# One decoder layer on one core: the seventh product of each weight pair moved behind the next pair's first, layer norm two pairs earlier, attention-output tiles rehoused

## The chip, the cores and the metric

The kernel runs on one core of one Trainium2 chip. The metric is device time in microseconds of one launch. The kernel before takes 1314.48 us, the median of three runs (1313.3 to 1315.68).

## What is computed

One layer of 1024 tokens by 1024 channels, float32, between two RMS norms. The normalised input `h` goes through one wide projection whose columns are cut into eleven pieces:

```python
h = _rmsnorm(x, norm_g)
q, k, v, o_pre, i_pre, f_pre, z_a, glu_in, z_b, ga_pre, gb_pre = split(h @ w_in)
q, k = silu(_causal_dwconv(concat(q, k), conv_qk_w, conv_qk_b))       # 4 taps
hm = _mlstm(q, k, v, i_pre + b_i, f_pre + b_f)                        # 4 heads of 256
out_a = sigmoid(o_pre) * headnorm(hm) * mhn_g * silu(z_a)
u = glu_in[..., :D_B] * sigmoid(glu_in[..., D_B:])
u = _causal_dwconv(u, dw_w, dw_b)                                     # 31 taps
u = silu(_layernorm(u, ln_g, ln_b)) * silu(z_b)
merged = sigmoid(ga_pre) * (out_a @ w_pa) + sigmoid(gb_pre) * (u @ w_pb)
out = _rmsnorm(x + merged @ w_out, final_g)
```

Every large matrix product is made exact to float32 by splitting each operand into a high and a low part and adding three passes (high by high, high by low, low by high).

## The kernel before, in words

**The projection.** `h` is turned, split and kept in SBUF as `hb`, four blocks of 512 inputs by 512 tokens, with three sums of blocks in `ext`. The columns of `w_in` are worked off in 40 jobs: the first six are four heads of `v` and the pairs gb0 and ga0 in plain form, and then come 34 "pairs" of 128-column tiles in the order of the table `ORDER` (jobs 6 to 39; names in the trace carry the job's number). `run_job` loads the raw weights of the next job, steps the generator `prep` of the next job (it splits the weights into `hi` and `lo`, the tags a, t, s and b standing for the weight blocks and for two pairs of sums; for t, s and b the low part is made on POOL's queue by an accumulating DMA), and issues the products of its own job in `quad`.

**A pair.** `quad` (L411) computes the four 512-token quarters of two column tiles from seven products instead of eight. `product` (L405, matmul L408) is twelve matmuls of 128 by 128 by 512 into one PSUM bank. In the order of the code: p1 into bank X, p2 into Z, p3 on top of X, p4 into W, p5 on top of X, p6 on top of Z, p7 on top of X. Between them X and Z are read out: ACT copies X after p1 (L431) and after p3 (L437) and Z after p2 (L434); DVE adds W (L441), then X after p5 (L445), then Z (L449). A product into a bank waits until the reader of that bank has finished, so p3 waits for L431, p5 for L437 and p7 for L445; between p5 and p7 stands p6 alone. `emit` then applies the pair's activation and stores.

**The 31-tap convolution.** The pairs ga0 to ga3 each give two tiles `u` to DVE, which needs 31 instructions of a whole tile each (L517 once, L519 30 times) into one accumulator `acc`; they are issued at low priority, so that the scheduler puts them where DVE has room. The accumulator is stored to `c_dram` (L520), and added into `s_dram` by an accumulating DMA on POOL's queue (L524). There is one `acc` buffer: the next tile's L517 waits until that DMA has read it.

**Layer norm** of the convolution, `layer_norm` (L595), is a generator that `run_job` steps beside a job's products, from pair `LN_AT` = 28 on (job 34). It loads the sum `s`, takes the mean on TensorE (`tstat`, `trow`), then goes twice over eight tiles: the first pass sums squares, the second scales each tile, applies SiLU, multiplies by `z` and stores to `u_dram`. A tile `ct` is loaded in `centred` (L589) and used at once. The tiles f, qr, qa and `z` share the tag `tmp` of five buffers.

**mLSTM and the last three products.** `stages` (L893) issues 16 chunks (four heads by four), whose outputs `gate` are stored to `oa_dram` (L884). Between stages `y_b` (L908) issues matmuls of yb, eight tiles, each multiplied by sgb (L912) and stored to `m1_dram`. When the chunks are done, `oa_tile` (L941) loads each of eight tiles `oar` from `oa_dram` and splits it into `oa` (ACT, L106, then DVE, L107). `oar` shares the tag `st`, two buffers, with sgb and sga. Then follow ya (`oa` by w_pa), `mrg`, and out (by w_out) with the final norm.

Instructions of one engine run in the order in which the Tile scheduler has put them; DMAs are issued by SP in its order, accumulating ones by POOL. PSUM is held as four banks `ms`, and four banks `qb` while the pairs run.

Of the kernel before, what the change touches and what calls it, by code (L numbers as in the profile page):

```python
# [9 lines left out]
F32 = mybir.dt.float32  # L10
F32R = mybir.dt.float32r
AF = mybir.ActivationFunctionType
ALU = mybir.AluOpType
# [28 lines left out]
         "zb0 zb1 zb2 zb3 o3 za3 mb3 ma3")  # L42
LN_AT = 28


@with_exitstack
def kernel(ctx: ExitStack, tc: tile.TileContext, x, norm_g, w_in, b_if, conv_qk_w, conv_qk_b,
# [13 lines left out]
    dpool = ctx.enter_context(tc.tile_pool(name="dpool", bufs=1, space=DRAM))  # L61
    ms_pool = ctx.enter_context(tc.tile_pool(name="ms_pool", bufs=4, space=PSUM))
    pj_cm, pj_pool = pool("pj_pool", bufs=2, space=PSUM)
    state = {}
    state["pj"] = pj_pool

# [344 lines left out]
    def quad(n, dst, emit):  # L411
# [17 lines left out]
        product(X, a11, b11, True, False)  # L429
        yield  # L430
        nc.scalar.copy(dst(0, 0), X)  # L431
        product(Z, s1, t1, True, False)
# [17 lines left out]
        emit(0, 1, dst(0, 1), False)  # L450
        product(X, a22, t4, False, True)
        yield
        emit(1, 0, X, True)

# [133 lines left out]

    def centred(c, n):  # L589
        ct = state["cv"].tile([P, KD - 1 + S], F32, tag="u", name=f"ct{n}_{c}", bufs=2)[:, 0:S]  # L590
        nc.sync.dma_start(ct, c_dram[c])
        nc.vector.tensor_tensor(ct, ct, state["mu"], op=ALU.subtract)
        return ct

    def layer_norm():  # L595
# [8 lines left out]
        mu = state["cv"].tile([P, S], F32, tag="acc", name="mu", bufs=1)  # L604
        state["mu"] = mu
        to_row(st, 0, mu)
        yield
        yield
        for c in range(KT):
            ct = centred(c, 0)  # L610
            if c == 0:
                nc.scalar.activation(sv, ct, AF.Square)
            else:
                nc.scalar.activation(ct, ct, AF.Square)
                nc.vector.tensor_tensor(sv, sv, ct, op=ALU.add)
            yield
# [5 lines left out]
        to_row(st, 1, sv)  # L622
        yield
        for c in range(KT):
            ct = centred(c, 1)
            z = state["tmp"].tile([P, S], F32, tag="tmp", name=f"z{c}", bufs=5)
            nc.sync.dma_start(z, z_dram[c])
            nc.vector.tensor_tensor(ct, ct, sv, op=ALU.mult)
            nc.scalar.activation(ct, ct, AF.Silu, bias=lb(c), scale=lg(c))
            nc.vector.tensor_tensor(z, z, ct, op=ALU.mult)  # L630
            nc.sync.dma_start(u_dram[c], z)
            yield
# [29 lines left out]
    close(pj_cm)  # L662
    qb_cm, state["qb"] = pool("qb", bufs=4, space=PSUM)
    lns_cm, lns = pool("lns", reuse_waits="tile")
# [225 lines left out]
    def stages():  # L890

        at = lambda i, s: chunks[i][s] if 0 <= i < len(chunks) else None
        for i in range(len(chunks) + 2):  # L893
            for f in (at(i - 1, "v"), at(i - 1, "u"), at(i + 2, "l"), at(i, "s"), None, at(i, "k"), at(i + 1, "p"), None,
                      at(i - 2, "f"), None, at(i, "i")):
                yield f

    u2 = []

    def u2_tile(c):  # L900
# [4 lines left out]
        u2.append(ut)  # L905

    def y_b():
        for d in range(KT):  # L908
            sg = yp.tile([P, S], F32, tag="st", name=f"sgb{d}", bufs=2)
            nc.sync.dma_start(sg, sgb_dram[d])  # L910
            ps = yield from proj(d, f"yb{d}", rhs=lambda k, sl: (u2[k][:, 0, sl], u2[k][:, 1, sl]))
            nc.vector.tensor_tensor(sg, ps, sg, op=ALU.mult)  # L912
            nc.sync.dma_start(m1_dram[d], sg)

# [53 lines left out]
    for d in range(KT):  # L968
        i = KT + d
        sg = yp.tile([P, S], F32, tag="st", name=f"sga{d}", bufs=2)  # L970
        nc.sync.dma_start(sg, sga_dram[d])
        m1 = yp.tile([P, S], F32, tag="m1", name=f"m1_{d}", bufs=2)
        nc.sync.dma_start(m1, m1_dram[d])
        ps = run(proj(i, f"ya{d}", rhs=lambda k, sl: (oa[k][:, 0, sl], oa[k][:, 1, sl])), i)
        mt = u2p.tile([P, 2, S], F32R, tag="u2", name=f"mrg{d}", bufs=KT)
        for hf in range(2):
            sl = slice(hf * 512, (hf + 1) * 512)
            nc.vector.tensor_tensor(sg[:, sl], ps[:, sl], sg[:, sl], op=ALU.mult)  # L978
            nc.vector.tensor_tensor(sg[:, sl], sg[:, sl], m1[:, sl], op=ALU.add)
            split(mt[:, 0, sl], mt[:, 1, sl], sg[:, sl])  # L980
# [90 lines left out]
```

## Time and profile before

| | us |
|---|---|
| median of three runs | 1314.48 |
| profiled execution, whole | 1314.68 |
| its span | 1312.9 |
| PE busy | 1219.8 (93%) |
| DVE busy | 929.5 (71%) |
| ACT busy | 638.6 (49%) |
| POOL busy | 142.0 (11%) |
| DMA moved | 217.89 MB, mean 166 GB/s |
| mean granted TensorE clock | 0.971 |

Span is from the first to the last instruction; the 1.8 us between it and the whole time lie around it. A matmul's shown duration overlaps the next one's, so that products are measured from start to start. In rows of a timeline, a bracket at the end gives the time the engine sat idle before the row and what ended that. A clock of 1.00 is TensorE's level of 2.4 GHz, and 0.5 the level of 1.2 GHz; a mean between them says how the two were mixed.

### The profile page before, as it was taken

To read this page: it belongs to the slowest core of one execution; us is meant where nothing else is said; L and a number is where in the kernel's file an instruction comes from. 1 tells how busy PE (TensorE), PEld (TensorE's weight loads), DVE (VectorE), ACT (ScalarE), POOL (GpSimd) and SP (SyncE) were. 2 spreads that over 40 slices of the span, in tenths; PEclk is the share of its full clock that TensorE was granted. 3 is DMA by queue.
4 is the path that set the end of the run, shared out by engine and by line. 5 is a ranking of instruction groups with operands and counts; after the bars stand their busy time and mean duration, and the time that the engine had idled before them with its cause. 6 is when DMAs were issued, how large, how long until landed. Compare 5 with 4: busy or idle time off the path is not lost. (4 is left out here: it accounts for less than half of the span.)

```text
span 1312.9 us, 16737 instructions
## 1 busy us (share of the span) xinstructions
PE 1219.8 (93%) x6228; PEld 1019.6 (78%) x6228; DVE 929.5 (71%) x1207; ACT 638.6 (49%) x948; POOL 142.0 (11%) x252
## 2 busy tenths in 40 slices
PE   8999999999989999999989988786898998899996
PEld 7889987887777877877868867665787886688996
DVE  6699899469789898989889455746787753444442
ACT  6522356646554474645646455566655531321223
POOL 1100011111111111111101111001111110000002
PEclk9999999999999999999989998897999998999998
DMA  8201577756765777666666977978877535443403
GB/s 263 65 1 59 167 172 169 197 129 144 174 159 132 163 166 175 147 143 163 164 167 172 247 204 209 290 228 260 244 229 227 168 109 188 151 142 135 170 17 129
DMA packets 170640, 217.89 MB, mean 166 GB/s; under 512 B 10177, under 2 KB 135481, under 8 KB 170558
## 3 DMA queue, kind: packets, MB, share of 16 engines
q1 hardware_dynamic: 154862, 168.58, 40.4%
q0 software_dynamic: 15696, 48.24, 20.0%
q8 instruction: 49, 0.80, 0.2%
q14 instruction: 33, 0.27, 0.1%
HBM read 117.67 MB, written 54.55 MB: 131 GB/s over the span
## 5 line engine op out<-in xcount | busy, mean ns | idle before, releaser
L519 DVE SCALAR_TENSOR_TENSOR acc<-u,dww,acc 128x1024 f32<-128x1024 f32 x240 | 307.7, 1282 | 3.7
L116 PE MATMUL v<-hi,hb 128*128 128x256 f32 (+1 forms) x512 | 94.5, 288 | 2.4 <-ACT hb L106 1.9
L116 PE MATMUL ya<-oa,whi 128*128 128x512 f32 x256 | 86.2, 413 | 9.2 <-ACT oa L106 5.7
L116 PE MATMUL out<-whi,mrg 128*128 128x256 f32 x512 | 91.0, 281 | 0.0
L116 PE MATMUL yb<-u,whi 128*128 128x512 f32 x256 | 85.3, 410 | 3.0 <-ACT u L106 1.7
L116 PEld LDWEIGHTS v<-hi,hb 128*128 128x128 f32 x512 | 80.3, 193 | 3.5 <-ACT hb L106 2.5
L116 PEld LDWEIGHTS out<-whi,mrg 128*128 128x128 f32 x512 | 78.6, 188 | 0.0
L116 PE MATMUL out<-wlo,mrg 128*128 128x256 f32 x256 | 71.9, 281 | 0.0
L116 PE MATMUL v<-lo,hb 128*128 128x256 f32 (+1 forms) x256 | 71.2, 286 | 0.0
L116 PEld LDWEIGHTS ya<-oa,whi 128*128 128x128 f32 x256 | 49.0, 194 | 27.7 <-ACT oa L106 9.4
L467 ACT ACTIVATE f<-f 128x512 f32<-128x512 f32 x69 | 43.1, 630 | 39.3 <-DVE f L445 24.3
L106 ACT CAST whi<-wr 128x1024 fp32r<-128x1024 f32 x24 | 25.2, 1050 | 74.9 <-PE ya L116 57.4
L489 DVE SCALAR_TENSOR_TENSOR qa<-qr,par,qa 128x1023 f32<-128x1023 f32 (+2 forms) x48 | 59.5, 1279 | 0.0
L116 PEld LDWEIGHTS yb<-u,whi 128*128 128x128 f32 x256 | 45.7, 190 | 12.4 <-ACT u L106 2.3
L116 PE MATMUL ya<-oa,wlo 128*128 128x512 f32 x128 | 52.0, 406 | 0.0
L116 PE MATMUL yb<-u,wlo 128*128 128x512 f32 x128 | 50.5, 394 | 0.0
L116 PEld LDWEIGHTS v<-lo,hb 128*128 128x128 f32 x256 | 48.5, 193 | 0.0
L116 PEld LDWEIGHTS out<-wlo,mrg 128*128 128x128 f32 x256 | 48.2, 188 | 0.0
L212 DVE TENSOR_TENSOR sum<-raw 128x512 f32<-128x512 f32 x34 | 23.4, 689 | 34.7 <-ACT f L437 6.9
L978 DVE TENSOR_TENSOR sga<-ya,sga 128x512 f32<-128x512 f32 x16 | 10.3, 686 | 45.9 <-PE ya L116 45.9
L208 DVE TENSOR_TENSOR sum<-raw 128x512 f32<-128x512 f32 x34 | 23.4, 689 | 24.9 <-ACT lo10b L193 3.5
L1023 ACT ACTIVATE junk<-res 128x256 f32<-128x256 f32 x32 | 13.4, 418 | 48.9 <-DVE res L1022 42.4
(1561 smaller groups left out, 3373.2 us busy)
## 6 DMA issues: line engine op xcount, KB each, us to landing
raw<-in_w_in_dram SPq DMA_DIRECT2D x144, 256.0 KB, 4.0
ct<-c_dram SPq DMA_DIRECT2D x16, 512.0 KB, 5.3
xt<-in_x_dram SPq DMA_DIRECT2D x8, 512.0 KB, 4.3
raw<-in_w_in_dram SPq DMA_DIRECT2D x8, 512.0 KB
v_dram<-vt SPq DMA_DIRECT2D x8, 512.0 KB, 2.9
c_dram<-acc SPq DMA_DIRECT2D x8, 512.0 KB
q_dram<-qa SPq DMA_DIRECT2D x8, 512.0 KB
sgb_dram<-f SPq DMA_DIRECT2D x8, 512.0 KB, 8.3
```

Of the source, the lines that this page charges most:

```text
L106: ins = nc.scalar.copy(hi, src)
L116: nc.tensor.matmul(ps, a, b, start=(first and j == 0), stop=(last and j == len(todo) - 1))
L208: nc.vector.tensor_tensor(sm[0][:, 0], raw[:, 0], raw[:, 3], op=ALU.add)
L212: nc.vector.tensor_tensor(sm[1][:, 0], raw[:, 0], raw[:, 1], op=ALU.add)
L467: nc.scalar.activation(t[j][:, HF[hf]], src, func, scale=sgn(neg))
L489: nc.vector.scalar_tensor_tensor(acc[j][:, s:], raw[j][:, 0:S - s], cw(KQ - 1 - s, t), acc[j][:, s:], op0=ALU.mult, op1=ALU.add)
L519: nc.vector.scalar_tensor_tensor(acc, u[:, k:k + S], dw(k, c), acc, op0=ALU.mult, op1=ALU.add)
L978: nc.vector.tensor_tensor(sg[:, sl], ps[:, sl], sg[:, sl], op=ALU.mult)
L1023: nc.scalar.activation(junk, r, AF.Square, accum_out=ss[:, t, n:n + 1])
```

## The change

Four things, all in the one function.

1. `quad` no longer issues p7. It leaves a closure `tail` (p7 and the emit of that quarter), which the next pair calls after its own p1. To let X live on beside the next pair's X, Z and W, `qb` gets six banks; `ms` has two in that time (`ms2_pool`), and four again after it (`ms3_pool`).
2. `LN_AT` is 26, so layer norm is stepped from job 32 on; `load_c` issues the loads of `ct` and `z` one step ahead of their use. Layer norm has one less step per pair to advance in, since a pair has one yield less.
3. The `oa` tiles get places of their own in reverse order, `oar` gets two buffers of its own, the first three `oa_tile` are issued as soon as the chunks' pools are closed, and yb's tiles 6 and 7 stay in SBUF (`m1k`) instead of going through `m1_dram`.
4. `stages` ends one round earlier and issues the last chunk's finish straight behind.

```diff
-LN_AT = 28
+LN_AT = 26
...
         product(X, a11, b11, True, False)
         yield
+        if state["tail"]:
+            state["tail"]()
         nc.scalar.copy(dst(0, 0), X)
...
-        product(X, a22, t4, False, True)
-        yield
-        emit(1, 0, X, True)
+
+        def tail():
+            product(X, a22, t4, False, True)
+            emit(1, 0, X, True)
+        state["tail"] = tail
...
-    def centred(c, n):
+    def load_c(c, n):
+        if c >= KT:
+            return None, None
         ct = state["cv"].tile([P, KD - 1 + S], F32, tag="u", name=f"ct{n}_{c}", bufs=2)[:, 0:S]
         nc.sync.dma_start(ct, c_dram[c])
-        nc.vector.tensor_tensor(ct, ct, state["mu"], op=ALU.subtract)
-        return ct
+        z = None
+        if n:
+            z = state["tmp"].tile([P, S], F32, tag="tmp", name=f"z{c}", bufs=5)
+            nc.sync.dma_start(z, z_dram[c])
+        return ct, z
...
+        ahead = load_c(0, 1)
         for c in range(KT):
-            ct = centred(c, 1)
-            z = state["tmp"].tile([P, S], F32, tag="tmp", name=f"z{c}", bufs=5)
-            nc.sync.dma_start(z, z_dram[c])
+            ct, z = ahead
+            ahead = load_c(c + 1, 1)
+            nc.vector.tensor_tensor(ct, ct, mu, op=ALU.subtract)
...
-    qb_cm, state["qb"] = pool("qb", bufs=4, space=PSUM)
+    close(ms_cm)
+    ms_cm, state["ms"] = pool("ms2_pool", bufs=2, space=PSUM)
+    qb_cm, state["qb"] = pool("qb", bufs=6, space=PSUM)
...
-        for i in range(len(chunks) + 2):
+        for i in range(len(chunks) + 1):
...
+        yield chunks[-1]["f"]
...
+            if state.get("oap"):
+                m1[d] = state["oap"].tile([P, S], F32, name=f"m1k{d}")
+                nc.vector.tensor_tensor(m1[d], ps, sg, op=ALU.mult)
+            else:
...
-    oa = [None] * KT
+    state["oap"] = oap
+    oa = [oap.tile([P, 2, S], F32R, name=f"oa{d}") for d in range(KT - 1, -1, -1)][::-1]
 
     def oa_tile(d):
-        oa[d] = oap.tile([P, 2, S], F32R, name=f"oa{d}")
-        raw = yp.tile([P, S], F32, tag="st", name=f"oar{d}", bufs=2)
+        raw = oap.tile([P, S], F32, tag="oar", name=f"oar{d}", bufs=2)
...
+    for _ in range(3):
+        oa_tile(todo.pop(0))
```

How the instructions move, in three places. First PE where pair 15 (k1) ends and pair 16 (mb1) begins, x, z and w being the banks X, Z and W of the pair whose number they carry; before:

```order
L408 MATMUL z15_2955<-hb_98,hi15s_2916 128x512 x2
L408 MATMUL z15_2955<-hb_98,lo15s_2917 128x512
L408 MATMUL x15_2954<-ext_779,hi15b_2937 128x512 x2
L408 MATMUL x15_2954<-ext_779,lo15b_2938 128x512
...
L408 MATMUL x16_3092<-hb_98,hi16a_3008 128x512 x2
L408 MATMUL x16_3092<-hb_98,lo16a_3009 128x512
```

and in the change:

```order
L407 MATMUL z15_2944<-hb_98,lo15s_2921 128x512
L407 MATMUL x16_3077<-hb_98,hi16a_3012 128x512 x2
L407 MATMUL x16_3077<-hb_98,lo16a_3013 128x512
...
L407 MATMUL x15_2943<-ext_783,hi15b_2929 128x512 x2
L407 MATMUL x15_2943<-ext_783,lo15b_2930 128x512
...
L407 MATMUL z16_3078<-hb_98,hi16t_3033 128x512 x2
L407 MATMUL z16_3078<-hb_98,lo16t_3034 128x512
...
L407 MATMUL w16_3137<-hb_98,hi16a_3012 128x512 x2
L407 MATMUL x16_3077<-ext_783,hi16t_3033 128x512 x2
```

Product p7 of pair 15 (x15 from hi15b and lo15b) now stands behind pair 16's p1, and so does every pair's. The last two rows show a second move: the first two matmuls of w stand ahead of p3, which the scheduler does in seven pairs (7, 13, 16, 21, 24, 28 and 31). On DVE the start of the next accumulator (L517 before, L520 now) stands ahead of the read of X after p5 in pair 15, as before; in pair 22, where it also stood ahead, it now stands behind.

Second, PE where the mean of the convolution is taken (tstat0, from the loaded sum s1); before, in pair 34 (zb2):

```order
L408 MATMUL w34_5662<-hb_98,hi34a_5541 128x512 x2
L408 MATMUL w34_5662<-hb_98,lo34a_5542 128x512
L577 MATMUL tstat0_5683<-ones_86,s1_5659 128x2 x8
L408 MATMUL x34_5618<-ext_779,hi34s_5584 128x512 x2
L408 MATMUL x34_5618<-ext_779,lo34s_5585 128x512
```

and in the change, where pair 34 begins:

```order
L407 MATMUL z33_5499<-hb_98,lo33s_5479 128x512
L407 MATMUL x34_5650<-hb_98,hi34a_5572 128x512 x2
L580 MATMUL tstat0_5425<-ones_86,s1_5401 128x2 x8
L407 MATMUL x34_5650<-hb_98,lo34a_5573 128x512
L407 MATMUL x34_5650<-hb_98,hi34a_5572 128x512
L586 MATMUL trow0_5458<-ident_81,tst0_5434 8x128
```

The mean has moved from behind p4 of pair 34 into its p1, ahead of p7 of pair 33.

Third, SP where the oa tiles are loaded; before:

```order
L884 DMA oa_dram_71<-gate2_3_8703 128x2x256
L913 DMA m1_dram_74<-sgb6_8839 128x1024
L703 DMA wr11_9103<-in_w_pa_dram 128x8x128
L943 DMA oar0_8979<-oa_dram_71 128x1024
L884 DMA oa_dram_71<-gate3_3_8817 128x2x256
L913 DMA m1_dram_74<-sgb7_8906 128x1024
L943 DMA oar1_8986<-oa_dram_71 128x1024
L703 DMA wr12_9171<-in_w_pa_dram 128x8x128
L943 DMA oar2_8991<-oa_dram_71 128x1024
```

and in the change:

```order
L900 DMA oa_dram_71<-gate2_3_8711 128x2x256
L900 DMA oa_dram_71<-gate3_3_8825 128x2x256
L966 DMA oar0_8917<-oa_dram_71 128x1024
L966 DMA oar1_8921<-oa_dram_71 128x1024
L996 DMA sga0_9028<-sga_dram_72 128x1024
L719 DMA wr11_9111<-in_w_pa_dram 128x8x128
L966 DMA oar2_8925<-oa_dram_71 128x1024
L966 DMA oar3_8935<-oa_dram_71 128x1024
L966 DMA oar4_8945<-oa_dram_71 128x1024
L996 DMA sga1_9096<-sga_dram_72 128x1024
L719 DMA wr12_9179<-in_w_pa_dram 128x8x128
L966 DMA oar5_8955<-oa_dram_71 128x1024
```

The last two chunks' stores stand next to each other, the loads of oar stand ahead of what waits for yb's last tiles (the stores to m1_dram of tiles 6 and 7 are gone), and the loads of sga0 and sga1 and of the weights wr11 and wr12 stand between them.

## Rows read from the trace of the kernel before

**Rows 1.** Windows: stretch, length, PE, PEld, DVE, ACT, POOL busy, PEclk, DMA share, GB/s
```profile
162.88:736.66 573.78, 553.54 (x2354) 443.68 (x2353) 487.37 (x504) 320.42 (x407) 80.76 (x96) 0.99 0.68 163
736.66:888.05 151.39, 129.96 (x539) 102.53 (x537) 79.29 (x88) 84.26 (x104) 16.40 (x18) 0.93 0.82 234
...
1105.60:1132.53 26.93, 17.89 (x44) 9.59 (x44) 11.95 (x10) 8.23 (x8) 0.00 (x0) 0.75 0.60 194
```

**Rows 2.** Waits of PE at L408: us in total, times, longest us
```profile
PE x L408 <- DVE qr L445: 11.7, 5, 5.1
PE x L408 <- DVE f L445: 10.1, 6, 3.8
```

**Rows 3.** Timeline of PE, p7 of pairs 15, 30, 33; what follows
```profile
364.62 1.22 PE L408 MATMUL x<-ext,hi15b 128*128 128x512 f32 x2 [5.08 <-DVE qr L445]
...
368.87 0.63 PE L408 MATMUL x<-hb,hi16a 128*128 128x512 f32 x2
...
672.75 1.22 PE L408 MATMUL x<-ext,hi30b 128*128 128x512 f32 x2 [4.04 <-DVE qr L445]
...
678.04 0.71 PE L408 MATMUL x<-hb,hi31a 128*128 128x512 f32 x2
...
733.86 0.63 PE L408 MATMUL x<-ext,hi33b 128*128 128x512 f32 x2
...
736.66 0.63 PE L408 MATMUL x<-hb,hi34a 128*128 128x512 f32 x2
```

**Rows 4.** Waits of DVE at L517
```profile
DVE acc L517 <- DMA s_dram<-acc: 17.1, 5, 7.1
```

**Rows 5.** Timeline of DVE in pair 15
```profile
361.83 0.81 DVE L517 TENSOR_SCALAR acc<-u,dww,par 128x1024 f32<-128x1024 f32 x1 [7.09 <-DMA s_dram<-acc]
```

**Rows 6.** Timelines of POOL and SP, from the convolution's end
```profile
728.51 0.87 POOL L524 DMA_DIRECT2D s_dram<-acc  x1 [8.27 <-DVE acc L519]
735.32 0.34 SPq L599 DMA_DIRECT2D s<-s_dram  x1
738.56 0.87 POOL L194 DMA_DIRECT2D lo34b<-raw  x1 [0.96 <-DMA s<-s_dram]
```

**Rows 7.** Timeline of PE, the waits of pairs 35, 36 and 39
```profile
767.17 1.22 PE L408 MATMUL x<-ext,hi35t 128*128 128x512 f32 x2 [3.54 <-ACT f L431]
774.74 0.72 PE L408 MATMUL x<-ext,hi35s 128*128 128x512 f32 x2 [0.32 <-ACT f L437]
781.55 0.73 PE L408 MATMUL x<-ext,hi35b 128*128 128x512 f32 x2 [1.01 <-DVE f L445]
806.97 1.22 PE L408 MATMUL x<-ext,hi36b 128*128 128x512 f32 x2 [3.80 <-DVE f L445]
847.71 0.80 PE L408 MATMUL x<-hb,lo39a 128*128 128x512 f32 x1 [5.92 <-DVE lo39a L107]
872.22 0.75 PE L408 MATMUL x<-ext,hi39t 128*128 128x512 f32 x2 [3.21 <-ACT f L431]
880.80 0.73 PE L408 MATMUL x<-ext,hi39s 128*128 128x512 f32 x2 [2.58 <-ACT f L437]
```

**Rows 8.** Instructions of the tile ct, second pass of layer norm: ns, first and last start
```profile
L630 DVE TENSOR_TENSOR z<-z,ct x8: 1218/1226/1226, 824.2 to 878.4; 128x1024 f32<-128x1024 f32 x8
```

**Rows 9.** Windows, columns as in rows 1, in the second pass
```profile
825.00:875.00 50.00, 39.83 (x157) 31.00 (x156) 30.45 (x32) 31.70 (x36) 5.17 (x6) 0.91 0.93 285
```

**Rows 10.** Timelines of DVE and SP, from chunk 14's gate to the oa tiles
```profile
1086.84 0.88 DVE L882 SCALAR_TENSOR_TENSOR gate<-op,par,gate 128x256 f32<-128x256 f32 x2 [2.28 <-PE op L880]
1101.28 0.88 DVE L882 SCALAR_TENSOR_TENSOR gate<-op,par,gate 128x256 f32<-128x256 f32 x2 [5.08 <-PE op L880]
1105.48 1.23 DVE L912 TENSOR_TENSOR sgb<-yb,sgb 128x1024 f32<-128x1024 f32 x1 [3.33 <-PE yb L116]
1109.55 17.70 SPq L943 DMA_DIRECT2D oar<-oa_dram  x6
```

**Rows 11.** The chain of waits in order of time: start, us, what
```profile
1132.53 79.60 PE ya L116 x340
```

More of the change, by code (lines that the diff above doesn't have):

```diff
@@ L61 @@
     dpool = ctx.enter_context(tc.tile_pool(name="dpool", bufs=1, space=DRAM))
-    ms_pool = ctx.enter_context(tc.tile_pool(name="ms_pool", bufs=4, space=PSUM))
+    ms_cm, ms_pool = pool("ms_pool", bufs=4, space=PSUM)
     pj_cm, pj_pool = pool("pj_pool", bufs=2, space=PSUM)
-    state = {}
-    state["pj"] = pj_pool
+    state = {"pj": pj_pool, "ms": ms_pool, "tail": None}
     def pj(name):
@@ L70, in ms @@
     def ms(name, shape=None):
-        return ms_pool.tile(shape or [P, 512], F32, tag="ms", name=name)
+        return state["ms"].tile(shape or [P, 512], F32, tag="ms", name=name)
     dram = lambda name, shape: dpool.tile(shape, F32, name=name)
@@ L604, in layer_norm @@
         mu = state["cv"].tile([P, S], F32, tag="acc", name="mu", bufs=1)
-        state["mu"] = mu
         to_row(st, 0, mu)
@@ L608, in layer_norm @@
         yield
+        ahead = load_c(0, 0)
         for c in range(KT):
-            ct = centred(c, 0)
+            ct = ahead[0]
+            ahead = load_c(c + 1, 0)
+            nc.vector.tensor_tensor(ct, ct, mu, op=ALU.subtract)
             if c == 0:
@@ L623, in layer_norm @@
         yield
+        ahead = load_c(0, 1)
         for c in range(KT):
-            ct = centred(c, 1)
-            z = state["tmp"].tile([P, S], F32, tag="tmp", name=f"z{c}", bufs=5)
-            nc.sync.dma_start(z, z_dram[c])
+            ct, z = ahead
+            ahead = load_c(c + 1, 1)
+            nc.vector.tensor_tensor(ct, ct, mu, op=ALU.subtract)
             nc.vector.tensor_tensor(ct, ct, sv, op=ALU.mult)
@@ L680 @@
         run_job(n, *([ln] if n >= 6 + LN_AT else []))
+    state["tail"]()
     for _ in ln:
@@ L687 @@
     close(qb_cm)
+    close(ms_cm)
     close(wq_cm)
     close(hb_cm)
+    ms_cm, state["ms"] = pool("ms3_pool", bufs=4, space=PSUM)
     pj_cm, state["pj"] = pool("pj2_pool", bufs=2, space=PSUM)
@@ L905, in u2_tile @@
         u2.append(ut)
+    m1 = [None] * KT
     def y_b():
@@ L911, in y_b @@
             ps = yield from proj(d, f"yb{d}", rhs=lambda k, sl: (u2[k][:, 0, sl], u2[k][:, 1, sl]))
-            nc.vector.tensor_tensor(sg, ps, sg, op=ALU.mult)
-            nc.sync.dma_start(m1_dram[d], sg)
+            if state.get("oap"):
+                m1[d] = state["oap"].tile([P, S], F32, name=f"m1k{d}")
+                nc.vector.tensor_tensor(m1[d], ps, sg, op=ALU.mult)
+            else:
+                nc.vector.tensor_tensor(sg, ps, sg, op=ALU.mult)
+                nc.sync.dma_start(m1_dram[d], sg)
     chunks[0]["l"]()
@@ L971 @@
         nc.sync.dma_start(sg, sga_dram[d])
-        m1 = yp.tile([P, S], F32, tag="m1", name=f"m1_{d}", bufs=2)
-        nc.sync.dma_start(m1, m1_dram[d])
+        if m1[d] is None:
+            m1[d] = yp.tile([P, S], F32, tag="m1", name=f"m1_{d}", bufs=2)
+            nc.sync.dma_start(m1[d], m1_dram[d])
         ps = run(proj(i, f"ya{d}", rhs=lambda k, sl: (oa[k][:, 0, sl], oa[k][:, 1, sl])), i)
@@ L978 @@
             nc.vector.tensor_tensor(sg[:, sl], ps[:, sl], sg[:, sl], op=ALU.mult)
-            nc.vector.tensor_tensor(sg[:, sl], sg[:, sl], m1[:, sl], op=ALU.add)
+            nc.vector.tensor_tensor(sg[:, sl], sg[:, sl], m1[d][:, sl], op=ALU.add)
             split(mt[:, 0, sl], mt[:, 1, sl], sg[:, sl])
@@ L1041 @@
     close(pj_cm)
+    close(ms_cm)
 _INS = ['x', 'norm_g', 'w_in', 'b_if', 'conv_qk_w', 'conv_qk_b', 'mhn_g', 'dw_w', 'dw_b', 'ln_g', 'ln_b',
```

## The prediction

> **What bounds it now.** I read the windows first. In the stretch of pairs 6 to 33 PE is busy 553.5 of 573.8 us at a clock of 0.99, with DVE next at 487.4; in pairs 34 to 39 it is busy 130.0 of 151.4, with DMA at 0.82 of its time; in the stretch where oa is made PE has 17.9 of 26.9 [rows 1]. So PE is the limit, and what can be won is what PE waits. A product stands 2.80 us from start to start (733.86 to 736.66) [rows 3], and a pair of seven about 19.5.
>
> In the waits of PE, the read of X after p5 (L445) is the largest cause: 11.7 + 10.1 = 21.8 us, in 11 places [rows 2]. Most is in few of them: 5.08 in pair 15, 4.04 in pair 30 [rows 3], 3.80 in pair 36 and 1.01 in pair 35 [rows 7]. In pair 15 the read is late because DVE, in order, stood 7.09 us at L517, which waited until the accumulating DMA had read `acc` [rows 5]; DVE stands 17.1 us there in all [rows 4]. After such a gap the clock falls to its lower level of 1.2 GHz for a part of the next product: pair 15's p7 takes 364.62 to 368.87 = 4.25 us, pair 30's 672.75 to 678.04 = 5.29 [rows 3], that is 1.45 and 2.49 more than 2.80.
>
> **Pairs 6 to 33: p7 behind the next p1.** The read at L445 had one product, p6, to hide behind; now it has p6 and the next pair's p1, 2.80 us more. Removed: 21.8 - 3.80 - 1.01 = 17.0 us of waits, and the half-clock excess of pair 15 (1.45), of pair 30 (2.49) and of pair 22, which I take as pair 15's (1.45): 5.4. Together 22.4. What stays: in pair 15 the accumulator's start is still ahead of the read, so 5.08 - 2.80 = 2.3; pair 30, 4.04 - 2.80 = 1.2; one fall of the clock after them, 1.45, between none and two. What comes: in seven pairs the order puts two matmuls of w ahead of p3, because it reckons with a late copy (L431). No p3 waits there today; the nearest rows are 0.32 and 3.54 in pair 35 [rows 7], so this is between 0 and 7 x 3.54 = 24.8. I take 7 x 0.32 = 2.2, since the 3.54 stands where DMA is at 0.82 and f tiles wait for their stores, and here DMA is at 0.68 [rows 1]. Gain 22.4 - 2.3 - 1.2 - 1.45 - 2.2 = **15.2**, with 22.4 as the upper end, and some 5 as the lower (three waits of 3.54 at the p3).
>
> Behind p7 stands emit of one quarter: its ACT instruction and the store come one product later, and SP's store of f too. They are covered by the next pair's products; without that cover the f slot is late for the pair after, which is the p3 wait just priced. The two `ms` banks serve only tstat, trow and the gates' small matmuls; at the start I put 0, at most some 1 us either way. The last pair's p7 stands alone at the end, as it did.
>
> **Pairs 34 to 39 and layer norm.** Gone or shorter: the wait of 36's p7 (3.80 becomes 3.80 - 2.80 = 1.0) and of 35's (1.01); and in pair 39 the waits of 5.92, 3.21 and 2.58 [rows 7]. These last lie beside the second pass, whose last step on DVE is now at 878.4, inside pair 39 [rows 8], with DMA at 0.93 of its time and 285 GB/s [rows 9]. Stepped from two pairs earlier, but by four steps a pair instead of five, and with loads one step ahead, the pass ends about one pair, 19.5 us, earlier, near 860: 39's waits at 872.22 and 880.80 lie behind that, and the one at 847.71 I count as gone too, since two thirds of the pass are then over. Sum 3.80 + 1.01 + 5.92 + 3.21 + 2.58 = 16.5, one fall of the clock with them 1.45, less the 1.0 that stays: 17.0.
>
> Against it stands a new wait. tstat0 now lies in p1 of pair 34, ahead of p7 of pair 33; in the clock of before that p1 would begin at 733.86 [rows 3] and tstat0 two matmuls later, near 734.3. But the convolution's last tile is accumulated from 728.51, the load of s begins at 735.32 when that has landed, and s is there at 738.5 (POOL's next wait ends on it) [rows 6]. PE stands 4.2 us with p1, p7 and all else queued behind, and pays one fall of the clock, 1.45: 5.7. DVE, which then makes the mean and waits for mu, is off PE's path for that pair. Net 17.0 - 5.7 = **11.3**. Ends: 20.5 if tstat0 hardly waits and 35's 3.54 goes too; -2 if 39's 5.92 stays and `tmp` costs two waits like 3.54.
>
> The trace's accumulate takes 735.32 - 728.51 = 6.8 us [rows 6]. The Trainium skill (DMA: Bandwidth & Descriptors, "Anatomy of one DMA — SWDGE (gpsimd) path") fits such a transfer at 2.0 us plus its bytes by 436e3, which for 512 KB would be an estimated 3.2; tstat0 would then stand 0.6 and the clock not fall, and the total below would be 5 lower, near 1271. The row was measured on this very transfer and decides.
>
> **The oa tiles.** Now oar's loads from the third on are issued 17.4 us apart from first to last, 3.47 each, the last at 1126.9 [rows 10], and PE goes on at 1132.53, 5.6 later, with 340 matmuls of ya in 79.60 us [rows 11]; only 44 of the 384 are done by then [rows 1]. After: on PE the last chunk's op matmuls stand 9 rows behind chunk 14's instead of 41, so its gate, now 1101.28 against 1086.84 [rows 10], comes at 1086.84 + 14.4 x 9/41 = 1090, and oar0 and oar1 start near 1091. Six gaps of 3.47 give the last load at 1111.8, and its low part at 1117.4. Ahead of oar5, due at 1104.9, SP has sga1's load, which needs the buffer that yb's last tile leaves at 1105.48 + 1.23 = 1106.7 [rows 10], and the load of weights behind it, one split (1.2) later: 1107.9, 3.0 late. So 1120.4 instead of 1132.5: **12.1**. 44 matmuls must stand ahead of it anyway, at 79.60/340 = 0.234 each 10.3 us, so that from 1105.6 it can't be before 1115.9: at most 16.6. At least some 8, if SP is held once more by as much. The stores and loads of yb's tiles 6 and 7 that go leave SP's queue, and are in these numbers.
>
> **Sum.** 15.2 + 11.3 + 12.1 = 38.6. Against the profiled execution's 1314.7 (the median is 0.2 lower) this is **1276.1 us**. A measurement of this kernel tells about 0.2%, 2.6 us, from no change.
>
> **Rivals.**
> *DVE holds the convolution's end.* PE gets ahead in pairs 6 to 33, but the convolution's steps, 31 a tile, don't end earlier, and PE gives all back at tstat0. For it: DVE is busy 487 of 574 us, and its order still has L517 ahead of reads. Against: 86 us idle, 17.1 of them at L517 alone [rows 4]. The first term goes: 1314.7 - 11.3 - 12.1 = 1291.3. Chance 0.20.
>
> *Everything comes off.* The upper ends: 22.4 + 20.5 + 16.6 = 59.5, 1255.2. For it: pair 22's accumulator start stands behind the read, and the two passes' loads are ahead. Against: tstat0's place. Chance 0.14.
>
> *The tmp tiles run out* (slower). z is fetched one step ahead and holds two of five `tmp` tiles, with o3's gate two more, so f tiles of pairs 36 to 39 come late and p3 and p5 of each wait as p3 of pair 35 does: eight waits of 3.54 + 1.45 = 40, with 39's 3.21 and 2.58 among them. The second term becomes 17.0 - 5.8 - 5.7 - (40 - 5.8) = -28.7, and the time 1314.7 - 15.2 - 12.1 + 28.7 = 1316.1; with the same at pair 35, two more, 1326. It decides from some ten such waits, or eight with 39's 5.92 kept (1322). Against it: only two such waits of over 3 us today, with the same five tiles. Chance 0.06 for slower.
>
> *The banks cost clock* (slower). If going round six banks left PE idle at each of the 34 pair ends and the clock fell, 34 x 1.45 = 49, so 1325. The rows speak against it: X of pair 34 follows pair 33's p7 with no idle [rows 3], at a clock of 0.99 over the stretch [rows 1]. Chance 0.01, in the slower 0.06. The Trainium skill (TensorE: Matmul & The Clock Gate, "A second HAM failure mode: psum-queue depth-cycling") has seen a kernel's clock go up and down through cycling PSUM banks; no row here shows it.
>
> That the change doesn't do what it says can be left out: the order shows each p7 moved.
>
> **Numbers.** The forecast's own case has 0.58, no change 0.02. Faster 0.58 + 0.20 + 0.14 = 0.92, same 0.02, slower 0.06. The range leaves out slower, same and half of the best case (0.15): from 1258, a little over the best case, to 1300, where DVE holds and the other two terms come to 15.
>
> **What would show it.** Right: waits at the read of X below 6 us in all, no product at half clock in pairs 22 and 36, a wait of some 4 us of tstat0 on the load of s, the last oa near 1120 in the clock of before, pair 39 without waits over 1 us. Wrong: p3 waits on ACT in pairs 7 to 31, a wait of tstat0 over 10 us (DVE holds), or p3 and p5 of pairs 36 to 39 waiting on ACT (tmp). The forecast falls if the sum of waits in pairs 6 to 33 is as large as now.

## The result, and the profile after

The changed kernel takes 1298.38 us, the median of four runs (1295.27 to 1302.29), beside 1315.08 for the kernel before in the same comparison (1313.3 to 1316.14). The ratio is 0.9876, with a 95% interval of 0.9844 to 0.9908: faster by 1.2%, some 16 us, where 2.9%, 38.6 us, were forecast. The time lies inside the range of 1258 to 1300. One launch of run 11 below took 3023.88 us and is left out of that run's median.

The profiled execution took 1299.98 us, with a span of 1297.9 against 1312.9. Cut at the first matmul of pair 6, of pair 34, of sc, of ya, and where ya goes on after the last oa tile, the 15.0 us lie so. In the kernel before, the start of p7 of pair 33 (733.86 [rows 3]) is the cut for pair 34, because that is the slot which p1 of pair 34 takes in the new order.

| stretch | before | after | difference | forecast |
|---|---|---|---|---|
| start to pair 6 | 162.9 | 166.2 | +3.3 | 0 |
| pairs 6 to 33 | 571.0 | 561.5 | -9.5 | -15.2 |
| pairs 34 to 39, to the first sc | 162.1 | 166.1 | +4.0 | -11.3 |
| chunks and yb, to the first ya | 209.65 | 206.2 | -3.4 | 0 |
| ya until the last oa tile | 26.9 | 17.5 | -9.4 | -12.1 |
| the rest | 180.4 | 180.4 | 0.0 | 0 |

The windows of the changed kernel at these cuts (length, busy time of PE, PEld, DVE, ACT and POOL, PE's clock, DMA's share, GB/s), to be read beside [rows 1]:

```profile
166.20:727.71 561.51, 545.95 (x2342) 437.12 (x2341) 485.53 (x503) 315.86 (x401) 79.77 (x95) 1.00 0.69 164
727.71:893.80 166.09, 135.13 (x552) 106.55 (x550) 81.81 (x94) 86.70 (x111) 18.19 (x27) 0.89 0.81 235
893.80:1100.00 206.20, 188.00 (x1121) 162.42 (x1121) 147.04 (x325) 107.42 (x239) 24.18 (x90) 0.97 0.68 211
1100.00:1117.51 17.51, 13.44 (x46) 9.30 (x44) 8.46 (x8) 6.15 (x6) 0.00 (x0) 0.81 0.53 180
```

In pairs 6 to 33 the clock now stands at its upper level throughout, 1.00; in pairs 34 to 39 it has gone down from 0.93 [rows 1] to 0.89, and the longest gap inside these pairs is now 8.1 us, where it was 5.92 [rows 7]. The waits of PE (us in total, times, longest) say which:

```profile
PE x L407 <- ACT f L432: 12.0, 8, 4.2
PE sc L115 <- ACT kh L105: 8.5, 1, 8.5
PE tstat L580 <- DMA s<-s_dram: 8.1, 1, 8.1
PE x L407 <- ACT f L438: 5.6, 3, 4.3
...
PE x L407 <- DVE qr L446: 2.9, 3, 1.3
...
PE gT L370 <- DVE gst L358: 2.2, 1, 2.2
...
PE x L407 <- DVE f L446: 0.4, 1, 0.4
```

The read of X after p5, 21.8 us before [rows 2], is down to 2.9 + 0.4. In its place stand the copies of X on ACT after p1 and after p3 (L432, L438), 17.6 us, where there were 9.7, and tstat0 (the mean's first matmuls, waiting for the loaded sum s). sc, the first matmul of chunk 0, waits 8.5 for kh, the split of that chunk's k, as it did before (7.9). What the p7 move was to do it did; a good part of what was to be won by it went into new waits.

**The mean of the convolution.** The timelines of POOL, SP and PE at the end of the convolution, as [rows 6] has them for before:

```profile
725.89 0.87 POOL L527 DMA_DIRECT2D s_dram<-acc  x1 [8.07 <-DVE acc L522]
...
732.05 0.34 SPq L607 DMA_DIRECT2D s<-s_dram  x1
...
727.71 0.61 PE L407 MATMUL x<-hb,hi34a 128*128 128x512 f32 x2
736.42 3.57 PE L580 MATMUL tstat<-ones,s 128*128 128x2 f32 x16 [8.10 <-DMA s<-s_dram]
739.86 0.77 PE L407 MATMUL x<-hb,lo34a 128*128 128x512 f32 x1
```

PE reaches p1 of pair 34 at 727.71, 6.2 us ahead of the slot's 733.86; the last accumulate goes out at 725.89, only 2.6 ahead of 728.51. The rest PE waits: 8.1 us, and sixteen small matmuls then take 3.57 at a granted clock of 0.50, where run 5 below shows 1.95 for them at 1.00. DVE has no room to be earlier. From the start of the last tile's steps to the accumulate:

```profile
660.39:725.60 65.21, 61.12 (x261) 48.32 (x260) 61.21 (x62) 34.80 (x45) 7.83 (x9) 1.00 0.70 176
```

DVE is busy 61.2 of 65.2 us. The average over the whole stretch, 487 of 574, which the forecast held against this, hides that its end is full.

**The copies of X.** ACT's timeline as pair 16 begins, and the p3 that waits:

```profile
368.94 0.59 ACT L501 ACTIVATE qr<-x 128x512 f32<-128x512 f32 x1
369.43 0.62 ACT L192 ACTIVATE lo16b<-hi16b 128x512 fp32r<-128x512 f32 x1
369.95 1.23 ACT L490 ACTIVATE qa<-qr,par 128x1024 f32<-128x1024 f32 x1
371.09 0.57 ACT L432 COPY f<-x 128x512 f32<-128x512 f32 x1
...
371.71 0.50 PE L407 MATMUL x<-ext,hi16t 128*128 128x512 f32 x1 [1.24 <-ACT f L432]
```

The emit of pair 15's p7 (L501) and the first step of its 4-tap convolution (L490) stand ahead of the copy on ACT. They did so before too, but then they ran beside pair 16's p1; now p1 is done before p7 begins (364.19), and the copy could have followed it. It repeats after six of the eight q and k pairs: p3 waits in pairs 9, 16, 21, 24, 28 and 31, 6.0 us in all.

**Pairs 35 and 37**, on PE and on ACT:

```profile
779.59 0.80 PE L407 MATMUL x<-ext,hi35s 128*128 128x512 f32 x1 [4.26 <-ACT f L438]
...
829.01 1.22 PE L407 MATMUL x<-ext,hi37t 128*128 128x512 f32 x2 [4.15 <-ACT f L432]
...
778.01 1.06 ACT L624 ACTIVATE ct<-ct 128x1024 f32<-128x1024 f32 x1 [2.60 <-DVE ct L620]
778.97 0.57 ACT L438 COPY f<-x 128x512 f32<-128x512 f32 x1
...
828.37 0.59 ACT L432 COPY f<-x 128x512 f32<-128x512 f32 x1 [4.30 <-DMA u_dram<-z]
```

Pair 39, whose three waits were 11.7 us [rows 7], waits 0.9 now. But pair 37's copy needs a `tmp` tile that a z holds until its store is done, and pair 35's stands on ACT behind a step of the first pass, for which ACT itself had waited 2.60 us idle. The second pass does end near the 860 of the forecast: its last step on DVE starts at 857.7.

**The oa tiles.** SP's loads and the chain's end, beside [rows 10, 11]:

```profile
1086.29 0.82 SPq L966 DMA_DIRECT2D oar<-oa_dram  x2
...
1101.45 0.32 SPq L996 DMA_DIRECT2D sga<-sga_dram  x1
...
1103.71 8.53 SPq L966 DMA_DIRECT2D oar<-oa_dram  x3
...
1117.51 79.59 PE ya L115 x340
```

The loads begin 13.7 us before ya's first matmul, and SP stands at sga1 until 1101.45, as reckoned; 340 matmuls remain as before.

### The profile page after: what moved, and what is told of

The parts are those of the page before. It is cut to its first block, busy times and chain, and to the rows that moved or that the text cites. A ratio compares the mean times of both kernels' runs of the same rounds, so it can differ in the third digit from the quotient of the medians.

```text
span 1297.9 us, 16700 instructions
## 1 busy us (share of the span) xinstructions
PE 1212.1 (93%) x6228; PEld 1015.8 (78%) x6228; DVE 927.9 (71%) x1207; ACT 631.9 (49%) x944; POOL 142.4 (11%) x252
## 5 line engine op out<-in xcount | busy, mean ns | idle before, releaser
L115 PE MATMUL ya<-oa,whi 128*128 128x512 f32 x256 | 83.1, 404 | 4.1 <-ACT oa L105 3.5
L1048 DVE TENSOR_TENSOR res<-out,res 128x256 f32<-128x256 f32 x32 | 13.4, 424 | 33.5 <-PE out L115 33.2
```

The lines of the kernel that those rows point to most:

```text
L115: nc.tensor.matmul(ps, a, b, start=(first and j == 0), stop=(last and j == len(todo) - 1))
L1048: nc.vector.tensor_tensor(r, ps[:, 0:DH], r, op=ALU.add)
```

## The experiments

The 95% intervals are of the ratio to the kernel before. "Stretch" is from the first product of pair 34 to the first sc, 166.1 in the changed kernel's profile.

**1. The copy of X first.**

```diff
-        if state["tail"]:
-            state["tail"]()
         nc.scalar.copy(dst(0, 0), X)
+        if state["tail"]:
+            state["tail"]()
```

> The copy of X after p1 is issued ahead of the previous pair's p7 and its emit; nothing else differs from the changed kernel. Theory (the copy stands on ACT behind the emit of p7 and the first step of that pair's 4-tap convolution): the waits of p3 on this copy in pairs 6 to 33, 7.0 us of the 12.0 in all, fall below 1.5, and pairs 6 to 33 (first product of pair 6 to first of pair 34) take 554 to 556 us instead of 561.5. Rival (VectorE holds the convolution's end): the wait of tstat0 on the load of s grows from 8.1 to 13 or more and the time stays within 3 us of the changed kernel's 1298; if VectorE does not hold it, the wait stays at about 8 and the time is 1291 to 1293.

Measured: 1295.16 us (0.9780 to 0.9876). The waits of p3 in pairs 6 to 33 are gone, but p5 waits instead. Waits of PE:

```profile
PE x L407 <- ACT f L438: 10.0, 6, 3.5
PE tstat L580 <- DMA s<-s_dram: 8.9, 1, 8.9
...
PE x L407 <- ACT f L430: 6.3, 2, 4.7
```

Pairs 6 to 33 take 559.5, 2.0 less, not 6 (the waits of p3 there came to 6.0 us, not the 7.0 of the expectation). One profile doesn't show these 2.0, since the changed kernel's second one, of run 8, has 559.8; but they hold over all: 557.8 to 559.5 in the seven profiles with the copy first, 559.8 to 561.5 in the seven others with p7 moved (runs 2 and 5 left out). The place on ACT was read rightly, but the work that a q or k pair's p7 brings has only moved one copy further. tstat0's wait rose by 0.8 only, and the time lies between the two theories: within their noise it is the changed kernel.

**2. Four banks each until pair 6.**

```diff
-    close(ms_cm)
-    ms_cm, state["ms"] = pool("ms2_pool", bufs=2, space=PSUM)
-    qb_cm, state["qb"] = pool("qb", bufs=6, space=PSUM)
+    qb_cm, state["qb"] = pool("qb4", bufs=4, space=PSUM)
...
+    close(qb_cm)
+    close(ms_cm)
+    ms_cm, state["ms"] = pool("ms2_pool", bufs=2, space=PSUM)
+    qb_cm, state["qb"] = pool("qb", bufs=6, space=PSUM)
     ln = layer_norm()
```

> The changed kernel with four banks each until pair 6 and two and six only from there. Theory (two banks for the gates' small matmuls hold the start up): the wait of gT on gst falls from 2.2 back to about 1.3 us, pair 6 begins near 163 instead of 166.2, and the time is about 3 us less than the changed kernel's, near 1295. Rival (the plain pairs themselves run slower, or the pools' second change costs as much at pair 6): pair 6 begins at 166 or later.

Measured: 1299.44 us (0.9828 to 0.9906). The start was held up by the two banks: from PE's last wait on `hb` to the gates' transposes gT it takes 54.2 to 54.3 us in all five profiles with four banks there, this one among them, and 57.1 to 57.2 in the fifteen with two, 2.9 more. But pair 6 begins at 163.94, not 163, because the second change of the pools now costs a wait there:

```profile
PE x L407 <- ACT vt L319: 1.8, 1, 1.8
```

And pairs 6 to 33 take 564.8, 3.3 more, and tstat0 waits 11.6. What is won at the start is gone when pair 34 begins (728.75 against 727.71). That fits DVE's hold on the convolution's end; the waits that grew in between were not followed one by one.

**3. Layer norm from the 29th pair again, loads still ahead** (`LN_AT = 28`).

> The changed kernel with layer norm from the 29th pair again, its loads one step ahead as in the change. Theory (the earlier start costs what it was to save: tstat0 before its sum is there, 8.1 us, and tmp tiles held by z): tstat0 does not wait, and the stretch from the first product of pair 34 to the first matmul of the first chunk's sc falls from 166.1 to 155 to 160, time 1288 to 1293. Rival (the earlier start pays): waits of 3 us and more come back in pairs 38 and 39, the stretch takes 166 to 175, time 1298 to 1307.

Measured: 1294.91 us (0.9787 to 0.9876), stretch 158.5, no wait of tstat0. The earlier start costs the stretch some 8 us; the time is 2 us above what the theory had. Part of the gain is lost at once: sc now waits 12.4 us on kh instead of 8.5, since the last steps of layer norm stand before chunk 0's loads on SP.

**4. The p7 move alone** (kernel before, with `tail` and six banks).

> The kernel before with p7 behind the next p1 and six banks alone; layer norm and the oa tiles as before. Theory (the move is worth the 9.5 us of pairs 6 to 33 less 3.3 at the start, and the oa tiles the rest): pairs 6 to 33 take 561 to 562 instead of 571.0, the oa stretch stays at 26.9, and the time is 1302 to 1307. Rival (the whole gain comes from the other parts): 1312 or more.

Measured: 1302.41 us, a ratio of 0.9922 (0.9891 to 0.9953), nine runs between 1300.1 and 1310.5. Pairs 6 to 33 take 561.4, as in the whole change, in a profile of the slowest of the nine. The theory held. sc waits 14.2 us on kh here: with one step less per pair, layer norm's last multiplication by z starts at 887.2, where it was 878.4 [rows 8].

**5. Fewer taps.** The last six steps of each convolution tile are left out, so that this kernel's work is less than the reference's.

```diff
-                for k in range(1, KD):
+                for k in range(1, KD - 6):
```

> The changed kernel with 25 of the 31 taps: each of the eight convolution tiles leaves out its last six steps on VectorE (48 steps of 1.28 us, 61 us; the output is then not the reference's). The order puts tstat0 ahead of pair 33's first product. Theory (VectorE, which stands idle for only 3.5 of the 65 us before the convolution's end, sets when the sum is there): the convolution ends 12 us and more earlier against pair 6's start (559.7 in the changed kernel), tstat0 waits under 3 us, and pairs 34 to 39 up to the first sc, 166.1 now, take 150 to 158. Rival (the accumulating DMA and the load of s, or TensorE itself, set it): the wait of tstat0 stays at 6 to 9 us.

Measured: 1288.09 us, one run. The accumulate, the load of s, and tstat0:

```profile
685.06 0.87 POOL L527 DMA_DIRECT2D s_dram<-acc  x1 [1.75 <-DVE acc L522]
...
692.70 0.32 SPq L607 DMA_DIRECT2D s<-s_dram  x1
...
699.07 1.95 PE L580 MATMUL tstat<-ones,s 128*128 128x2 f32 x16 [1.72 <-DMA s<-s_dram]
```

The convolution ends 39 us earlier against pair 6, and tstat0 waits 1.7. DVE held the sum; the transfers took no less than in the changed kernel (7.6 us from the accumulate to the load, and 6.4 until PE goes on, beside 6.2 and 4.4). The stretch takes 154.7, 11.4 less than in the changed kernel, but part of that is that tstat0 now stands ahead of it, in pair 32. Against the 162.1 of the kernel before, 7.4 us are won, not the 11.3 of the forecast: the other waits in pairs 34 to 39 come to 18.4 us even so.

**6. The oa tiles alone** (kernel before, with this part's code).

> The kernel before with the oa tiles' part of the change alone (reverse places, own oar buffers, the last chunk's finish closed up, yb's tiles 6 and 7 kept). Theory (this part is independent of the rest): ya's 384 matmuls take 97 us instead of 106.35 from first to last, all before them stays within 1 us of the kernel before, and the time is 1304 to 1307. Rival (what is won there is given back by the chunks, because SP's order is another): 1310 or more.

Measured: 1305.38 us, 0.9920 (0.9892 to 0.9947). ya takes 96.5 and begins 0.5 us later than in the kernel before. The part is independent.

**7 and 8. The copy first and the 29th pair, and the changed kernel again beside it.**

> Both in one: the copy of X ahead of p7 (as in the first run of this study) and layer norm from the 29th pair with loads one step ahead. Theory (the copy is worth 2 us in pairs 6 to 33, the later start 4 to 8 in pairs 34 to 39, and the two do not touch each other): 1289 to 1294. Rival (the end of layer norm now sets when chunk 0's loads start, and takes what TensorE wins): the wait of sc on kh is 14 us or more and the time 1295 to 1298.

> The changed kernel once more, timed beside the others on this chip: 1295 to 1301, as in its own four runs.

Measured: 1291.63 us (0.9785 to 0.9848) against 1299.47 (0.9841 to 0.9904). The two edits add up: 7.8 us together, where they had 3.2 and 3.5 singly.

**9. Layer norm's part alone** (kernel before, `LN_AT = 26` and loads ahead).

> The kernel before with the layer norm's part of the change alone (from the 27th pair, loads one step ahead); p7 stays in its own pair. The order puts tstat0 ahead of pair 34's first product. Theory (the early start costs more than it gives, because the convolution's sum is not there): tstat0 waits 4 us or more, the stretch of pairs 34 to 39 up to the first sc is not shorter than the 159.3 of the kernel before, time 1313 to 1320. Rival (the early start pays as forecast, and it is the moved p7 that spoils it): waits of pair 39 gone, time 1302 to 1308.

Measured: 1337.95 us, a ratio of 1.0166 (1.0132 to 1.0201): slower by more than the theory had. Waits of PE from 736 on:

```profile
PE tstat L577 <- DMA s<-s_dram: 7.1, 1, 7.1
PE x L408 <- ACT hi38a L106: 6.0, 1, 6.0
PE x L408 <- ACT hi37a L106: 5.7, 1, 5.7
PE x L408 <- DVE lo38a L107: 5.1, 1, 5.1
PE x L408 <- ACT f L431: 4.5, 2, 2.6
```

Beside tstat0, pairs 37 and 38 wait for their own first weights (hi and lo of tag a). By itself this part of the change is a loss of 1.7%. In the whole change most of that does not appear; why p7's place covers it was not tried.

**10. z loaded at its use.**

```diff
-            ct, z = ahead
+            ct = ahead[0]
             ahead = load_c(c + 1, 1)
+            z = state["tmp"].tile([P, S], F32, tag="tmp", name=f"z{c}", bufs=5)
+            nc.sync.dma_start(z, z_dram[c])
```

> The changed kernel with z loaded in the step that uses it; only the tiles ct are loaded one step ahead. Theory (z, fetched one step ahead, holds two of the five tmp tiles, and the copy of X in pairs 37 and 38 waits for the store of a z): the waits of p3 on this copy in pairs 37 and 38 fall from 4.2 and 1.9 to 1.5 or less each, tstat0's stays, and pairs 34 to 39 up to the first sc take 158 to 163 instead of 166 to 168. Rival (the copy is late because DMA is slow there, whoever holds the tile): the two waits stay at 5 or more together.

Measured: 1298.11 us (0.9839 to 0.9888), stretch 165.1; p3 of pair 37 waits 5.7, of 38 1.6. The theory falls: the early load of z is not what makes the copy late.

**11. Layer norm wholly as before** (p7 and oa as changed).

> The changed kernel with layer norm as before (from the 29th pair, loads at use); p7 and the oa tiles as changed. Theory (layer norm's part of the change is a loss): faster than the changed kernel by 2 to 8 us, 1290 to 1296, and within 3 us of the run with the 29th pair and loads ahead (1294.9). Rival (loads one step ahead are worth it by themselves): 3 us or more slower than that run, 1298 or more.

Measured: 1296.20 us (0.9831 to 0.9885). In its profile the stretch is 157.7, but that was one of its two fastest executions (1293.4), and sc waits 13.6 behind it. The time is 0.2 above the theory's range and below the rival's, but the interval overlaps that of the changed kernel (0.9844 to 0.9908). Inconclusive.

**12. Layer norm stepped twice per product from pair 36 on** (on top of run 7).

> As the run with the copy first and the 29th pair (1291.6), but layer norm is stepped twice per product from pair 36 on. Theory (in that run the end of layer norm holds chunk 0's loads, so that sc waits 11.9 on kh): the wait of sc falls to 8 or so and the time to 1286 to 1290. Rival (tmp tiles and DMA hold the passes, so that the steps come as new waits of p3 and p5 in pairs 37 to 39): waits there grow by as much, time 1290 to 1295.

Measured: 1297.79 us (0.9839 to 0.9884), 6 slower than run 7. sc waits 7.4 as hoped, and pairs 35 to 39 wait 23 us in the place of it, where run 7 has 15: the rival, and more than its 1290 to 1295.

**13 and 14. o3 and za3 ahead of zb0 to zb3, and run 7 again.**

> As the run with the copy first and the 29th pair (1291.6), but the pairs o3 and za3 stand ahead of zb0 to zb3, so that o3's two gate tiles are given back before layer norm's second pass begins. Theory (with f tiles of two pairs, z's tiles and o3's gate the five tmp tiles run out, and the copies of X and Z in pairs 38 and 39 wait for a store): these waits, 2.2 + 1.1 + 2.4 us there, fall below 2 together, and pairs 34 to 39 up to the first sc take 152 to 157 instead of 159.6; time 1286 to 1290. Rival (DMA, or layer norm's own end, holds them whoever has the tiles): waits of ACT in pairs 37 to 39 stay above 4 us, or the wait of sc on kh grows above 14, and the time stays at 1290 to 1294.

> The run with the copy first and the 29th pair once more, beside the one above on the same chip: 1289 to 1296.

Measured: 1295.90 us (0.9846 to 0.9883) against 1291.85 (0.9808 to 0.9848). p5 of 38 and p3 and p5 of 39 wait 3.4, 3.1 and 3.5: the gate tiles are not it either. In these pairs DMA is at 0.81 to 0.86 of its time, at 234 to 239 GB/s, in the profiles of the kernel before, of the changed one and of runs 13 and 14 alike.

**15 and 16. The low parts on DVE in pairs 34 to 39**, in the changed kernel, and on top of run 7.

```diff
-            if tag in DMA_LOW and not j["plain"]:
+            if tag in DMA_LOW and not j["plain"] and n < 34:
```

> The changed kernel with the low parts of t, s and b of pairs 34 to 39 made by VectorE, as those of tag a are, instead of by ScalarE and an accumulating DMA: 18 transfers of up to 512 KB leave the DMA queues and the write and read of as much with them, and VectorE gets 18 subtractions. The order still has tstat0 in pair 34's p1. Theory (the copies of pairs 35 to 38 wait for tiles whose stores and loads are slow because DMA is at 0.81 of its time there): DMA's share in these pairs falls to 0.65 or less, the waits of p3 and p5 on ScalarE's copies there, 10.5 us now, fall below 5, that of tstat0 stays at 8 to 11, and pairs 34 to 39 up to the first sc take 155 to 161. Rival (it is ScalarE's and VectorE's order, steps of layer norm ahead of the copies, whatever the transfers take): waits stay at 8 or more, 163 to 168.

> The same in the fastest version so far (copy first, 29th pair, 1291.6 and 1291.9): theory, pairs 34 to 39 up to the first sc take 148 to 153 instead of 157.5 to 159.6, time 1281 to 1287. Rival (layer norm's end holds chunk 0's loads all the same): sc waits 14 or more on kh and the time is 1288 to 1293.

Measured: 1283.03 us (0.9732 to 0.9778) and **1265.92 us (0.9601 to 0.9647)**. The DMA queues (packets, MB, share of 16 engines) from 727 to 870, first of the changed kernel:

```profile
q1 hardware_dynamic: 15144, 27.89, 56.7%
q0 software_dynamic: 2528, 7.93, 29.4%
```

and of run 15, with its window below:

```profile
q1 hardware_dynamic: 15119, 28.32, 59.3%
q0 software_dynamic: 144, 0.52, 2.1%
```

```profile
727.00:870.00 143.00, 130.12 (x553) 104.19 (x551) 96.84 (x109) 69.36 (x88) 1.67 (x1) 0.95 0.62 202
```

DMA's share in this window falls from 0.86 to 0.62, and the waits of p3 and p5 there from 10.5 us to 2.8; tstat0's stays (7.2), as the order says. The stretch is 150.2, and 138.9 in run 16, where PE waits 0.2 us in all of these pairs and then 15.1 for kh; both are better than the theory had (155 to 161, 148 to 153). DVE, which got the subtractions, has room once the convolution is done. The same edit takes off ACT the copies that made the low parts ready, 1.05 + 1.05 + 0.62 us in each of six pairs, 16 us; how much of the gain is DMA's and how much ACT's these two runs don't tell. For DMA speaks that ACT was idle just ahead of the two long waits of the changed kernel, 4.30 us for a store in pair 37, and 2.60 in pair 35 for DVE, which had itself just stood 2.57 for the load of a ct and 1.39 for a low part's DMA.

**17. The same edit alone, in the kernel before.**

> The kernel before with the low parts of t, s and b of pairs 34 to 39 made by VectorE. Theory (DMA's load was what bounded pairs 34 to 39 already before the change, so that the forecast's second term had no room): pairs 34 to 39 up to the first sc take 140 to 150 instead of 159.3, DMA's share falls from 0.82 to 0.65, time 1298 to 1308. Rival (the load only binds with layer norm's new loads): 156 or more, time 1311 or more.

Measured: 1296.97 us, 0.9873 (0.9858 to 0.9888): this one line is worth as much as the whole change. The window of pairs 34 to 39:

```profile
736.00:880.00 144.00, 130.31 (x559) 104.08 (x557) 95.39 (x107) 72.39 (x91) 2.58 (x9) 0.95 0.61 201
```

The stretch takes 145.7 instead of 159.3: what this edit takes off cost as much before the change. But not all waits go with it. Those of PE from 736 to 887 are now

```profile
PE sc L116 <- ACT kh L106: 7.4, 1, 7.4
PE z L408 <- ACT f L434: 6.1, 1, 6.1
PE x L408 <- DVE lo39a L107: 4.0, 1, 4.0
PE x L408 <- ACT f L431: 1.2, 1, 1.2
PE x L408 <- ACT hi39a L106: 0.9, 1, 0.9
```

The waits of pairs 35 and 36 are gone; pair 39 still waits 12.3 us beside the second pass, as it did before (12.6), though DMA is at 0.71 there (830 to 868) instead of the 0.93 of [rows 9].

**18. Layer norm's steps doubled on top of run 16.**

> The fastest version so far (1265.9: copy first, 29th pair, low parts on VectorE in pairs 34 to 39) with layer norm stepped twice per product from pair 36 on. Theory (with DMA no longer full, the steps can run ahead, and the wait of sc on kh, 15.1, falls to some 8): 1257 to 1261. Rival (as when this was tried with the accumulating DMAs in place, the steps come back as waits of pairs 37 to 39): 1264 or more.

Measured: 1274.19 us (0.9676 to 0.9707), slower than run 16: sc waits 7.3, and pairs 38 and 39 take back more (4.0, 2.1 and 2.1 us and the clock with them). Run 16 is the fastest version of this study.

## Why the prediction came out as it did

**Pairs 6 to 33: right in kind, 9.5 of 15.2.** The 22.4 us of the read at L445 did go: 2.9 stay in pairs 15, 27 and 30 and 0.4 in pair 32, where 2.3 + 1.2 were put for pairs 15 and 30, and the fall of the clock put at 1.45 did not come. The mis-sized term is the p3 wait, taken as 7 x 0.32 = 2.2: it measured 0.2 to 1.3 in each of six places, 6.0 in all, with 1.1 at a p5 beside it. The range of the term held it (the lower end of the gain, put at some 5, comes to 6.9 by its own terms), the chosen row did not: 0.32 was the row of a p5, on the copy at L437, and not of a p3. The price was in sight in another way, the two instructions of the q and k pair that stand ahead of the copy on ACT and that p1 no longer covers. Beyond that, pairs 18, 25 and 31 have new waits of 0.5, 1.5 and 1.5.

**The start: 3.3 us, put at 0, at most some 1.** The two `ms` banks hold up the gates' small matmuls: 2.9 us up to gT (run 2), of which some 1 is gT's own wait (2.2 instead of 1.3). Pair 6 begins at 162.8 to 162.9 in all four profiles that keep four banks, at 163.9 in run 2, and at 164.0 to 167.4 in the others; what spreads these last by 3 us, with the same code up to there, is not known. The words "serve only" passed over a pool that was halved.

**Pairs 34 to 39: 4.0 us lost where 11.3 were to be won.** This is the step that failed. It said that tstat0 would stand 4.2 us, by carrying the times of before over as they are. PE had meanwhile gained 6.2 us on the clock, and the convolution's end only 2.6: the wait was 8.1 here and 11.1 in the run again. The rival "DVE holds the convolution's end" was right in its mechanism, as run 5 shows, and had 0.20; its price, the whole first term, did not come, since tstat0 took back 3.9 of the 9.5. It should have weighed more, since the last stretch of DVE is full in the kernel before too: from 660.39 to 728.13, 61.9 of 67.7 us. And the step said that 39's 11.7 us would go, because layer norm would be over: they went, but 4.3, 4.2 and 1.9 came in pairs 35, 37 and 38. All waits of PE inside these pairs but tstat0's, 21.3 us before, were to fall to 5.8; they fell to 14.3. So of the 15.3 us between forecast and result 8.5 are such waits, 3.9 are tstat0's longer wait, and the rest, 2.9, was not traced (the clock is 0.89 there instead of 0.93). The pass, moved earlier, took waits along. Its transfers are the likely reason, with DMA at 0.93 of its time and 285 GB/s in the row on which the step rested [rows 9]: runs 15 and 16 took load off DMA, and off ACT, and the waits of p3 and p5 went. That it is DMA and not ACT is argued, not shown, and pair 39 in run 17 shows that the edit alone, with layer norm as it was, does not do it everywhere. The rival on `tmp` tiles named the place (p3 and p5 of pairs 36 to 39), and pair 37's copy does wait for a tile; but runs 10 and 13 gave tiles back and won nothing. A sixth tile was not tried.

By the rule of the Trainium skill (DMA: Bandwidth & Descriptors, "Anatomy of one DMA — SWDGE (gpsimd) path") the accumulate was estimated at 3.2 us; from its issue to the load of s it took 6.2 here (725.89 to 732.05) and 7.6 in run 5. The row decided rightly.

**The oa tiles: 9.4 of 12.1.** The walk was right: the gate earlier, the loads in pairs, SP held at sga1. The 2.7 us that are missing lie in small pieces: the loads begin 13.7 us ahead of ya's first matmul where 14.6 had been put (0.9), SP gets past sga1 and the weights 17.4 us after the first load instead of 16.9 (0.5), and from there to the last low part it takes 13.8 instead of 12.5 (1.3).

**The banks cost clock: no.** With six banks the clock of pairs 6 to 33 is 1.00. What the Trainium skill (TensorE: Matmul & The Clock Gate, "A second HAM failure mode: psum-queue depth-cycling") reports of another kernel shows in no row here.

The chunks' 3.4 us are not explained: the stretch takes 204 to 212 us in these runs, and from 205 to 212 in those that all have the changed form of it.

The three parts, each alone, have ratios of 0.9922 (p7), 0.9920 (oa) and 1.0166 (layer norm). The first two together would give 0.984; run 11, which has just these two, has 0.9858 (0.9831 to 0.9885), and the whole 0.988.

## What to carry to other kernels

Before a wait is booked as gained, find what the next fixed date hangs on, and look at the engine that sets it in its last stretch rather than on average: here PE came 6.2 us earlier, and stood at the mean for a sum that DVE had ready only 2.6 earlier. Where waits end on loads and stores, as here with DMA at 0.81 to 0.86 of its time, moving work earlier can move its waits along; look first for bytes, or for transfers that cost more than their bytes, that an engine with room can take over. And where an emit is moved past another copy on the same engine, price it by the instructions that come to stand ahead of that copy, not by the smallest wait in sight.

## What was not expected of the hardware

Accumulating DMAs are dear for their bytes: in pairs 34 to 39 of the changed kernel they moved 7.93 MB and took 29.4% of the DMA engines' time, 3.7% a MB, beside 56.7% for 27.89 MB, 2.0% a MB, of the plain ones. Runs of one and the same kernel spread by up to 1.0% (1308.9 to 1321.6 in the twelve runs of the kernel before that stood beside runs 1 to 4), so that parts of 3 us could be read from stretches of a profile only, not from times; and the stretch of pairs 34 to 39 itself differs by 2 us between two profiles of one kernel (166.1 and 168.0, 159.6 and 157.5).
